# Modulation sums of the first layer on TensorE's column groups, inside the loop of the first projections

## The chip, the cores and the metric

The kernel runs on one core of a Trainium2 chip. The metric is device microseconds from one launch to its end; the median of 3 runs of the kernel before is 2728.34 us (2719.16 to 2734.02). One more execution was profiled: 2728.04 us, of which 2726.2 us lie between its first and its last instruction (the span), so 1.8 us lie around the span. All times below that carry a start are counted from the start of that span. TensorE does the matrix products (PE in the profile, its weight loads PEld), VectorE is DVE, ScalarE is ACT, GpSimd is POOL; SP issues most of the transfers (DMA) from the main memory.

## The reference

Two layers over x of 1024 positions by 2048 features, float32. Only the head of layer 0 is touched:

```python
cond = jax.nn.silu(c)                              # c: (1, 2048)
mod = cond @ w_mod[layer] + b_mod[layer]           # w_mod[0]: 2048 x 6144
shift, scale, gate = jnp.split(mod[:, None, :], 3, axis=-1)
h = rms_norm(x, ln_pre_g[layer]) * (1.0 + scale) + shift
...
proj = h @ w_in                                    # 2048 x 7168, parts a_u a_v a_z q k v b_z
out_a = spatial_gating(gelu(a_u), gelu(a_v), ...) * silu(a_z)
out_b = stick_breaking(q, k, v) * silu(b_z)        # 8 heads of 128, causal, 128-query blocks
x = x + gate * rms_norm(concat(out_a, out_b) @ w_out_ab, ln_post_g)
```

The shift part and the scale part of w_mod[0] are 2048 by 2048 numbers each, 16.8 MB each, and are read once for one vector times matrix product. Layer 1 (a state space layer) is not touched.

## The kernel before

Matrix products run at float32 accuracy by splitting both factors into a rounded part and a rest (`split`, L179: ACT makes the rounded part `whi`, DVE or POOL the rest `wlo`), and three products per tile (`mm3`, L205 to L208). h is kept transposed, features on the partitions, in two halves of 512 positions: `hTh[0]`, `hTl[0]` and `hTh[1]`, `hTl[1]`, 16 tiles k of 128 features each. A projection of 256 output columns takes its weights in pieces of 4 k (1024 numbers per partition, the tile `wraw`, 3 buffers), cut into two splits.

The head of the program, in its order:

1. The first half of x is loaded (`xa`, 4 transfers) and then six small vectors (`rows`), all by SP; one transpose makes columns of them, and ACT makes `cond`.
2. `x_norm` (L313): ACT squares and sums each of the 4 row blocks, `rstd_from` gives the factors, ACT and DVE scale.
3. The scale part of the modulation in six column groups (L352): 16 transfers of 1 MB through three slots of `raw0`; DVE multiplies each k row by `cond` and accumulates (`matvec`, L174); a product with a vector of ones sums over the partitions (`col_sums`, L158); `scale_shift` makes `asc`. Then `h_tile` (L327) transposes x, and ACT and DVE write hTh and hTl, without the shift. Between these groups the first half of six banks (three projections, called `first`: b_z of two heads, q with k, a_u with a_z) is accumulated, k by k, with weights that GpSimd's queue loads and whose rests GpSimd makes.
4. The second half of x (`xb`) is loaded, normed, transposed; the shift part of the modulation is summed by DVE in four column groups (L403, tiles `m`); the second half of the first two projections follows (`bz0e`, `qk0e`).
5. `add_shift` (L343) adds the shift to all 32 tiles of h and splits them again; what `first` lacked is repaired later: `bias_first` (L438) loads the six weight columns again and forms shift times weights on DVE, the products `pbias`, and biases for b_z, u, z, q, k.
6. `proj_v` of head 0 (`v0e`, both halves), the second half of the third projection (`uz0e`), and then the loop over the 8 heads: projections of the next head fill TensorE between the small steps of the attention of the current one (`z`, `oT`). The chunks of the other modulation parts run on DVE in heads 0 to 2 (`mod_chunk`).

The order on each engine is made by the scheduler of the framework from priorities (`hi_prio`) and the data's dependences. Each engine runs its list in order; SP and GpSimd issue transfers in order, and an issue that waits for a buffer holds all behind it.

Of the kernel before, what the change touches and what calls it, by code (L numbers as in the profile page):

```python
# [19 lines left out]
KT = 16  # L20
# [43 lines left out]
def hybrid_trunk(ctx: ExitStack, tc: tile.TileContext, x, c, ln_pre_g, ln_post_g, w_mod, b_mod,  # L64
# [52 lines left out]

    xa = big_tile(1, [128, 4, D], F32, "xa")
    for t in range(4):
        dma(out=xa[:, t, :], in_=x[0, t * 128:(t + 1) * 128, :])  # L120
    with tc.tile_pool(name="p0r", bufs=1) as p0r:
        rows = p0r.tile([128, 128], F32, name="rows")
        dma(out=rows[0:16], in_=flat_rows(c[0], 16))
        dma(out=rows[16:48], in_=ln_pre_g.rearrange("l (r p) -> (l r) p", p=128))
        for i in range(2):
            dma(out=rows[48 + 32 * i:80 + 32 * i], in_=flat_rows(b_mod[i, 0:4096], 32))
        dma(out=rows[112:120], in_=flat_rows(sgu_norm_g[0], 8))
        dma(out=rows[120:128], in_=flat_rows(b_glu[0], 8))
# [3 lines left out]
    tab.begin("silu")  # L132
    tab.act(cond, cols[:, 0:16], AF.Silu)
# [49 lines left out]
    def load_raw(parts, ncols, dma=dma):  # L183

        raw = wp.tile([128, RAW], F32, tag="wraw", name="wraw")
# [78 lines left out]
    pu = []  # L264
    pq_stack = ctx.enter_context(ExitStack())
    pq = pq_stack.enter_context(pool("pq"))
    wv0 = w_mod[0].rearrange("(k p) n -> p k n", p=128)
    bias0 = const.tile([128, 6], F32, name="bias0")

# [9 lines left out]
    def new_uz():  # L279
        st["u"], st["z"] = (pu[0].tile([128, L], F32, tag=n, name=n) for n in ("u", "zg"))  # L280

    def evac_bz(cb, hf, ps):
        S.activation(perm(st["bz"][cb])[:, hf * 64:(hf + 1) * 64, :], ps.rearrange("p (n j) -> p n j", j=8), AF.Copy)

    def evac_qk(cb, hf, ps):
        S.activation(st["qk"[cb]][:, hf * 512:(hf + 1) * 512], ps, AF.Copy,
                     scale=(1.0 / math.sqrt(HD) if cb == 0 else 1.0))

    def evac_qk0(cb, hf, ps):
        S.activation(st["qk"[cb]][:, hf * 512:(hf + 1) * 512], ps, AF.Copy)  # L290

    def evac_uz(cb, hf, ps):
        S.activation(st["uz"[cb]][:, hf * 512:(hf + 1) * 512], ps, AF.Copy)
# [9 lines left out]
    new_bz()  # L303
    new_qk()
    with pool("p0") as p0:
        tab.begin("explog")
        rb = big_tile(1, [128, 8192], F32, "raw0")
        hTh[0] = big_tile(0, [128, KT, 512], F32R, "hTh0")
        hTl[0] = big_tile(0, [128, KT, 512], F32R, "hTl0")
        xs_ = [[xa[:, t, :] for t in range(4)]]  # L310
        junk0 = p0.tile([128, D], F32, tag="xb", name="junk0", bufs=4)

        def x_norm(xt, junk, n):  # L313
            ss = p0.tile([128, 4], F32, tag=f"ss{n}", name=f"ss{n}")
            for t in range(4):
                S.activation(junk, xt[t], AF.Square, accum_out=ss[:, t:t + 1])
            r = rstd_from(ss, 4, D, p0, f"r{n}")
            for t in range(4):
                if t % 2 and n == 0:
                    V.tensor_scalar(out=xt[t], in0=xt[t], scalar1=r[:, t:t + 1], scalar2=None, op0=ALU.mult)  # L320
                else:
                    S.activation(xt[t], xt[t], AF.Copy, scale=r[:, t:t + 1])

        x_norm(xs_[0], junk0, 0)
        ps6 = [mm_tile("first") for _ in range(4)] + [ps_z.tile([128, 512], F32, tag="z", name="first") for _ in range(2)]

        def h_tile(hf, k):  # L327
            pz = xbank[k % 3] if hf and k % 3 < 2 else ps_t.tile([128, 512], F32, tag="t", name="xT")
            for i in range(4):
                T.transpose(pz[:, i * 128:(i + 1) * 128], xs_[hf][i][:, k * 128:(k + 1) * 128], ident)  # L330
            sc = asc[:, 0, k:k + 1]
            S.activation(hTh[hf][:, k, :], pz, AF.Copy, scale=sc)
            lo = hTl[hf][:, k, :]
            if hf == 0:
                V.scalar_tensor_tensor(out=lo, in0=pz, scalar=sc, in1=hTh[hf][:, k, :], op0=ALU.mult, op1=ALU.subtract)
            else:
                tmp = p0.tile([128, 512], F32, tag="ht", name="ht", bufs=2)
                S.activation(tmp, pz, AF.Copy, scale=sc)
                G.tensor_tensor(out=lo, in0=tmp, in1=hTh[hf][:, k, :], op=ALU.subtract)

        hsb = []

        def add_shift(hf, k):  # L343
            if not hsb:
                hsb.append(p0.tile([128, 4, 512], F32, tag="xb", name="hs", bufs=4))
            tmp = hsb[0][:, k % 4, :]
            V.scalar_tensor_tensor(out=tmp, in0=hTh[hf][:, k, :], scalar=shf[:, 0, k:k + 1], in1=hTl[hf][:, k, :],
                                   op0=ALU.add, op1=ALU.add)
            split(hTh[hf][:, k, :], hTl[hf][:, k, :], tmp, (V, G)[k % 2])

        nm = 0
        for kb, (ka, kz) in enumerate(((0, 1), (1, 2), (2, 4), (4, 8), (8, 12), (12, 16))):  # L352
            n = (kz - ka) * 128
            acc = rb[:, 6144 + (kb % 2) * 512:6144 + (kb % 2) * 512 + n]
            kn = 2048 // n
            for k0 in range(0, KT, kn):
                m = rb[:, (nm % 3) * 2048:(nm % 3 + 1) * 2048].rearrange("p (k n) -> p k n", k=kn)
                nm += 1
                last = dma(out=m, in_=wv0[:, k0:k0 + kn, D + ka * 128:D + kz * 128])
                for ki in range(kn):  # L360
                    matvec(acc, m[:, ki, :], k0 + ki)
            pcs = ps_o.tile([128, kz - ka], F32, tag="o", name="cs")
            col_sums(pcs, acc, kz - ka)
            scale_shift(0, slice(ka, kz), pcs, None, p0)
            with hi_prio():
                for k in range(ka, kz):
                    h_tile(0, k)
            if kb == 0:
                after = last.ins
                with hi_prio(), tc.issue_after(after):  # L370
                    raws = [load_raw(src_ab(*first[0], 0)(0, 4), 256)]
            if kb < 2:
                continue
            if kb == 2:
                with hi_prio(), tc.issue_after(last.ins):
                    raws += [load_raw(src_ab(*f_, 0)(0, 4), 256) for f_ in first[1:]]
            for gi, (s0, s1) in enumerate(first):
                k0 = kz - 4
                src = src_ab(s0, s1, 0)(k0, k0 + 4)
                for wh, wl in load_w(src, 256, G, raws[gi] if kb == 2 else None, G.dma_start):  # L380
                    for kk in range(2):
                        for cb in range(2):
                            mm3(ps6[gi * 2 + cb], *opT(k0 + kk, wh[:, kk], wl[:, kk], cb, 0), k0 + kk == 0, k0 + kk == KT - 1)
                    k0 += 2
        evs = (evac_bz, evac_qk0)
        for gi in range(2):
            for cb in range(2):
                with hi_prio():
# [939 lines left out]
```

## Time and profile before

| what | value |
|---|---|
| median of 3 runs | 2728.34 us |
| profiled execution, its span | 2728.04 us, 2726.2 us |
| TensorE busy in the span | 2595.3 us, 95% |
| VectorE busy | 1733.9 us, 64% |
| granted TensorE clock, mean | 0.986 of full speed |
| last product of `first` starts | 145.62 us |
| first product of `v0e`, of `uz0e` starts | 231.94 us, 286.99 us |

A matmul's record lasts longer than the time it holds the array, since the next one starts before it ends: the distance from one start to the next is the price when the array is full. A product of two float32 operands is two instructions in the trace, a product of split operands is one.

### The profile page before, as it was taken

Reading aid. Unit: us, or ns where it says so; the run is one execution under the profiler, and the core shown is the slowest. Engines: PE = TensorE matmul, PEld = TensorE weight load, DVE = VectorE, ACT = ScalarE, POOL = GpSimd, SP = SyncE. Lnnn points to the kernel's source line nnn. Section 1 sums busy time; section 2 is a strip of 40 time slices with the busy share of each in tenths; the row PEclk is TensorE's granted clock in tenths of the full one; section 3 lists DMA queues with packets and bytes.
Section 4 is the critical chain, followed back from the end, with each engine's and each line's share of the span. In section 5 each row is a group of like instructions: output and inputs, shape, how many; then the busy total and the mean of one; then the engine's idle time right before and its main releaser. Section 6 shows DMA issues by size and latency. Waiting matters only on the chain.

```text
span 2726.2 us, 38501 instructions
## 1 busy us (share of the span) xinstructions
PE 2595.3 (95%) x13639; PEld 2180.4 (80%) x13639; DVE 1733.9 (64%) x3783; ACT 1029.2 (38%) x2035; POOL 487.8 (18%) x771
## 2 busy tenths in 40 slices
PE   4878999999999999999999999999999999999998
PEld 3667988988988878878889777777877888887876
DVE  7798876666776666765847663455364768446354
ACT  3444552433424234334334353444352321134333
POOL 2375000000001162441613400020030000002000
PEclk9889999999999999999999999999999999999999
DMA  8764746375482232422413335453254676363354
GB/s 279 269 209 117 220 148 217 124 237 175 156 261 66 73 101 70 122 73 68 137 45 115 103 105 189 147 178 108 99 191 154 206 220 199 118 205 139 131 193 165
DMA packets 357311, 417.95 MB, mean 153 GB/s; under 512 B 23760, under 2 KB 239104, under 8 KB 355712
## 3 DMA queue, kind: packets, MB, share of 16 engines
q1 hardware_dynamic: 347568, 392.95, 45.1%
q0 software_dynamic: 9552, 22.56, 2.5%
q8 instruction: 107, 1.75, 0.3%
q14 instruction: 84, 0.69, 0.1%
HBM read 355.62 MB, written 59.79 MB: 152 GB/s over the span
## 4 chain that ended last, share of the span: by engine, by line
PE 68%; DVE 11%; DMA 8%; issue 8%; ACT 3%; POOL 1%; SPq 0%; DVEq 0%; ACTq 0%; POOLq 0%
PE oT L580 2%; PE z L552 2%; DVE acc L174 2%; DMA mraw<-in_w_mod_dram 2%; PE o0e L206 2%; PE o1e L206 2%; PE o1e L208 2%; PE o1e L207 2%; PE o0e L208 2%; PE o0e L207 2%; DVE wlo L181 1%; DMA xr<-in_x_dram 1%; DMA wraw<-cat_d 1%; PE su1e L206 1%; PE wT_ps L576 1%
## 5 line engine op out<-in xcount | busy, mean ns | idle before, releaser
L180 ACT ACTIVATE whi<-wraw 128x512 fp32r<-128x512 f32 x632 | 395.2, 629 | 997.8 <-PE o1e L208 91.3
L181 DVE TENSOR_TENSOR wlo<-wraw,whi 128x512 fp32r<-128x512 f32 x592 | 420.8, 714 | 486.3 <-ACT whi L180 482.6
L174 DVE SCALAR_TENSOR_TENSOR macc<-mraw,cond,macc 128x512 f32<-128x512 f32 x240 | 180.0, 750 | 67.3 <-DMA mraw<-in_w_mod_dram 62.9
L207 PE MATMUL o1e<-wlo,catH 128*128 128x512 f32 x256 | 101.1, 395 | 4.7 <-DVE wlo L181 4.5
L56 ACT ACTIVATE sp<-sp 128x128 f32<-128x128 f32 (+3 forms) x192 | 99.4, 521 | 3.7
L207 PE MATMUL o0e<-wlo,catH 128*128 128x512 f32 x256 | 100.7, 393 | 0.0
L208 PE MATMUL o1e<-whi,catL 128*128 128x512 f32 x256 | 100.5, 393 | 0.0
L208 PE MATMUL o0e<-whi,catL 128*128 128x512 f32 x256 | 100.2, 393 | 0.0
L206 PE MATMUL o0e<-whi,catH 128*128 128x512 f32 x256 | 90.9, 398 | 7.9 <-ACT whi L180 3.9
L904 POOL TENSOR_TENSOR gt<-gt,zt 128x1024 f32<-128x1024 f32 x8 | 20.0, 2511 | 430.6 <-DMA gt<-g_d 430.6
L206 PE MATMUL o1e<-whi,catH 128*128 128x512 f32 x256 | 88.1, 395 | 2.2 <-ACT jk L704 2.0
L56 ACT ACTIVATE sp<-z 128x128 f32<-128x128 f32 (+3 forms) x96 | 46.6, 486 | 110.0 <-PE z L552 109.0
L735 POOL DMA_DIRECT2D x_d<-y x32 | 17.9, 561 | 369.7 <-DVE y L732 368.3
L580 PE MATMUL oT<-wT,v 128*128 128x128 f32 x576 | 81.1, 277 | 0.7 <-DVE wT L578 0.7
L174 DVE SCALAR_TENSOR_TENSOR acc<-m,cond,acc 128x512 f32<-128x512 f32 x60 | 74.6, 1243 | 7.9 <-DMA m<-in_w_mod_dram 6.5
L580 PEld LDWEIGHTS oT<-wT,v 128*128 128x128 f32 x576 | 75.9, 193 | 4.0 <-DVE wT L578 1.1
L552 PE MATMUL z<-k,q 128*128 128x128 f32 (+3 forms) x192 | 77.3, 486 | 0.6 <-DVE wt L569 0.6
L56 ACT ACTIVATE wt<-wt 128x128 f32<-128x128 f32 (+3 forms) x96 | 50.2, 523 | 62.5 <-DVE wt L569 62.2
L557 DVE SCALAR_TENSOR_TENSOR sp<-z,sp 128x128 f32<-128x128 f32 (+3 forms) x96 | 52.9, 551 | 31.6 <-ACT sp L56 31.5
L181 POOL TENSOR_TENSOR wlo<-wraw,whi 128x512 fp32r<-128x512 f32 x40 | 59.8, 1510 | 65.9 <-ACT whi L180 64.4
L578 DVE COPY wT<-wT_ps 128x128 f32<-128x128 f32 (+3 forms) x96 | 53.1, 553 | 28.8 <-PE wT_ps L576 28.3
L559 POOL TENSOR_SCALAR_AFFINE_SELECT sp<-sp 128x128 f32<-128x128 f32 x64 | 25.3, 395 | 257.0 <-DVE sp L557 240.7
(634 smaller groups left out, 8100.1 us busy)
## 6 DMA issues: line engine op xcount, KB each, us to landing
wraw<-in_w_in_ab_dram SPq DMA_DIRECT2D x268, 256.0 KB, 3.3
mraw<-in_w_mod_dram SPq DMA_DIRECT2D x256, 256.0 KB, 3.7
wraw<-in_w_in_ssm_dram SPq DMA_DIRECT2D x56, 512.0 KB, 4.4
wraw<-in_w_out_ab_dram SPq DMA_DIRECT2D x48, 512.0 KB, 3.7
raw<-in_w_mod_dram SPq DMA_DIRECT2D x16, 1024.0 KB, 6.2
m<-in_w_mod_dram SPq DMA_DIRECT2D x32, 512.0 KB, 4.4
wraw<-in_w_out_ssm_dram SPq DMA_DIRECT2D x32, 512.0 KB, 3.7
wraw<-in_w_in_ab_dram SPq DMA_DIRECT2D x17, 512.0 KB, 4.8
```

The source lines that it names most:

```text
L56: r = self.nc.scalar.activation(out, in_, func, **kw)
L174: V.scalar_tensor_tensor(out=acc, in0=m, scalar=cond[:, k:k + 1], in1=acc, op0=ALU.mult, op1=ALU.add)
L180: S.activation(h, r, AF.Copy)
L181: eng.tensor_tensor(out=lo, in0=r, in1=h, op=ALU.subtract)
L206: T.matmul(ps, sh, mh, start=first, stop=False)
L207: T.matmul(ps, sh, ml, start=False, stop=False)
L208: T.matmul(ps, sl, mh, start=False, stop=last)
L552: T.matmul(z[:, :w], q[:, i * 128:(i + 1) * 128], kT[:, k0:k1], start=True, stop=True)
L557: V.scalar_tensor_tensor(out=a[:, :w], in0=z[:, :w], scalar=0.0, in1=a[:, :w], op0=ALU.max, op1=ALU.add)
L576: T.transpose(pt[:, j * 128:(j + 1) * 128], b[:, j * 128:(j + 1) * 128], ident)
L578: V.tensor_copy(wT[:, :w], pt[:, :w])
L580: T.matmul(oT, v[:, k0 // 128 + j, :], wT[:, j * 128:(j + 1) * 128], start=nb_done == 0, stop=nb_done == i)
```

## The change

Step 3 to 5 are rewritten. The condition vector is repeated 32 times in columns (`condb`, 128 x 16 x 32), and w_mod's rows are streamed through TensorE against it: four products of 32 output partitions, each in another column group of the array (`prow[32j:32j+32]`), the groups 0 and 1 for the scale (even and odd k), 2 and 3 for the shift. The row sums are copied by ACT (`srow`) and turned into columns by a product with a selecting matrix `sel`, which also adds the groups. Scale and shift of two k tiles (a block, 8 blocks in all) are so known together, and `h_tile` writes h with its shift: the repair by `add_shift` and `bias_first` goes, and so do `bias0` and the scaling that waited for it. A block takes 4 transfers of 1 MB in 8 slots (`rb` and `ring2`), and every second block takes three weight pieces (`load_raws`), which land in `wraw` or in the buffers of bz0, bz1 and k; all are issued by SP, two blocks ahead. The small vectors move to ACT's queue. PE, ACT, DVE and SP follow the written order in this loop (`manual_schedule`), all splits are on DVE. After it `v0e` of the first half is put ahead of `bz0e` and `qk0e`, and `v0e` of the second half behind them.

```diff
     xa = big_tile(1, [128, 4, D], F32, "xa")
-    for t in range(4):
-        dma(out=xa[:, t, :], in_=x[0, t * 128:(t + 1) * 128, :])
...
-        dma(out=rows[0:16], in_=flat_rows(c[0], 16))
+        S.dma_start(out=rows[0:16], in_=flat_rows(c[0], 16))
...
+        with tc.manual_schedule(engines={mybir.EngineType.SP}), hi_prio():
+            for t in range(4):
+                xlast = dma(out=xa[:, t, :], in_=x[0, t * 128:(t + 1) * 128, :])
...
-        def add_shift(hf, k):
...
+        def h_tile(hf, k, xt, pz):
...
+            S.activation(hi, pz, AF.Identity, scale=sc, bias=sh)
+            full = xt[:, :, cs]
+            S.activation(full, pz.rearrange("p (a b) -> p a b", a=4), AF.Identity, scale=sc, bias=sh)
+            V.tensor_tensor(out=hTl[hf][:, k, :].rearrange("p (a b) -> p a b", a=4), in0=full,
+                            in1=hi.rearrange("p (a b) -> p a b", a=4), op=ALU.subtract)
...
+        def load_chunks(b, half):
+            for i in range(2):
+                slot = (4 * b + 2 * half + i + 4) % 8
...
+                    st["last"] = dma(out=m, in_=wv0[:, half * 8:half * 8 + 8, c0:c0 + 256])
...
+        def sums(b, half):
+
+            for k in range(0, 8, 2):
+                for j in range(4):
+                    m = chunk[b, half, 1 - j // 2]
+                    kk = half * 8 + k + j % 2
+                    T.matmul(prow[32 * j:32 * j + 32], condb[:, kk, :], m[:, k + j % 2, :],
+                             start=kk < 2, stop=kk >= KT - 2)
...
+            for b in range(NB):
+                old = dict(wpair)
+                sums(b, 0)
+                if b + 2 < NB:
+                    load_chunks(b + 2, 0)
+                if b:
+                    for gi in range(3):
+                        first_mm(b - 1, 0, gi, old[gi])
+                sums(b, 1)
+                if b + 2 < NB:
+                    load_chunks(b + 2, 1)
+                    if b % 2 == 0:
+                        load_raws(b + 2)
+                srow = pu.tile([128, 256], F32, tag="u", name="srow")
+                S.activation(srow, prow, AF.Copy)
+                if b:
+                    first_mm(b - 1, 1, 0, old[0])
+                ks = slice(2 * b, 2 * b + 2)
+                cs = hd[:, 256:260].rearrange("p (k s) -> p k s", s=2)
+                for i in range(2):
+                    T.matmul(cs[:, i, :], srow[:, i * 128:(i + 1) * 128], sel, start=True, stop=True)
+                scale_shift(0, ks, cs[:, :, 0], cs[:, :, 1], p0)
+                split_w(b, 0)
+                h0(2 * b)
+                for gi in (1, 2):
+                    if b:
+                        first_mm(b - 1, 1, gi, old[gi])
+                    split_w(b, gi)
+                h0(2 * b + 1)
...
-        for kb in range(4):
-            acc = p0.tile([128, 512], F32, tag="acc", name="acc0", bufs=2)
...
+        proj_v(0, 0)
...
-        proj_T(0, *first[0], evac_bz, "bz", ((1,),), G)
-        proj_T(0, *first[1], evac_qk0, "qk", ((1,),), G)
-        for hf in range(2):
-            for k in range(KT):
-                add_shift(hf, k)
+        proj_T(0, *first[0], evac_bz, "bz", ((1,),))
+        proj_T(0, *first[1], evac_qk, "qk", ((1,),))
+        proj_v(0, 1)
...
-        def bias_first():
...
-        bias_first()
```

On PE, in the middle of the head: before, a group's column sums (`cs`), one transpose of x and then the products of `first` on that tile; numbers behind a name tell buffers apart.

```order
L207 MATMUL first<-hTl_136,whi 128x512
L208 MATMUL first<-hTh_135,wlo 128x512
L158 MATMUL cs<-ones,raw_134 128x1 x4
L206 MATMUL first<-hTh_135,whi 128x512 x4
L330 MATMUL xT<-ident,xa 128x128 x4
L207 MATMUL first<-hTl_136,whi 128x512
L208 MATMUL first<-hTh_135,wlo 128x512
```

And now, the middle of block 1: sums of its second half (`mrow`), products of block 0's second tile, the columns (`sel`), a transpose, and products again.

```order
L384 MATMUL mrow_154<-raw0_143,condb_147 32x256 x16
L213 MATMUL first_148<-hTh0_145,whi_250 128x512
L214 MATMUL first_148<-hTl0_146,whi_250 128x512
L215 MATMUL first_148<-hTh0_145,wlo_251 128x512
L213 MATMUL first_149<-hTh0_145,whi_250 128x512
L214 MATMUL first_149<-hTl0_146,whi_250 128x512
L215 MATMUL first_149<-hTh0_145,wlo_251 128x512
L436 MATMUL mrow_154<-sel_102,srow_332 128x2 x2
L353 MATMUL xT_350<-ident_91,xa_108 128x128 x4
L213 MATMUL first_150<-hTh0_145,whi_262 128x512
L214 MATMUL first_150<-hTl0_146,whi_262 128x512
L215 MATMUL first_150<-hTh0_145,wlo_263 128x512
```

The column sums were eight short instructions behind work of DVE; now 16 products of 32 output partitions each stand twice in a block between the products of `first`, and all of them use TensorE. The tile of which `first` is multiplied is one block older than the sums.

On DVE, at the same place: before, the accumulation of the modulation (L174) with the small steps and the rest of an h tile between.

```order
L174 SCALAR_TENSOR_TENSOR raw_134<-raw_134,cond 128x512 x4
L335 SCALAR_TENSOR_TENSOR hTl_136<-xT,asc,hTh_135 128x512
L174 SCALAR_TENSOR_TENSOR raw_134<-raw_134,cond 128x512 x7
L172 TENSOR_SCALAR raw_134<-raw_134,cond 128x512
L174 SCALAR_TENSOR_TENSOR raw_134<-raw_134,cond 128x512 x3
L164 TENSOR_TENSOR sct<-cs,cols 128x4
L174 SCALAR_TENSOR_TENSOR raw_134<-raw_134,cond 128x512
L165 SCALAR_TENSOR_TENSOR asc<-sct,cols 128x4
L174 SCALAR_TENSOR_TENSOR raw_134<-raw_134,cond 128x512
L335 SCALAR_TENSOR_TENSOR hTl_136<-xT,asc,hTh_135 128x512
```

Now, one block: the columns of scale and shift, three rests of weights, two rests of h.

```order
L170 TENSOR_TENSOR sct<-mrow,cols 128x2
L171 SCALAR_TENSOR_TENSOR asc<-sct,cols 128x2
L174 TENSOR_TENSOR shf<-mrow,cols 128x2
L187 TENSOR_TENSOR wlo<-wraw,whi 128x512
L359 TENSOR_TENSOR hTl_146<-xa,hTh_145 128x512
L187 TENSOR_TENSOR wlo<-wraw,whi 128x512 x2
L359 TENSOR_TENSOR hTl_146<-xa,hTh_145 128x512
```

No accumulation is left on DVE there; the rests of the weights have come to it from POOL.

On SP, from the start: before, x, the small vectors, then the modulation's chunks with the first weight pieces between.

```order
L120 DMA xa<-in_x_dram 128x2048 x4
L123 DMA rows<-in_c_dram 16x128
L124 DMA rows<-in_ln_pre_g_dram 32x128
L126 DMA rows<-in_b_mod_dram 32x128 x2
L127 DMA rows<-in_sgu_norm_g_dram 8x128
L128 DMA rows<-in_b_glu_dram 8x128
L359 DMA raw_134<-in_w_mod_dram 128x16x128
L188 DMA wraw<-in_w_in_ab_dram 128x4x256
L359 DMA raw_134<-in_w_mod_dram 128x16x128
L359 DMA raw_134<-in_w_mod_dram 128x8x256 x2
L188 DMA wraw<-in_w_in_ab_dram 128x4x128 x4
L359 DMA raw_134<-in_w_mod_dram 128x4x512 x12
```

Now:

```order
L136 DMA xa<-in_x_dram 128x2048 x4
L375 DMA ring_144<-in_w_mod_dram 128x8x256 x4
L195 DMA wraw<-in_w_in_ab_dram 128x4x256
L195 DMA wraw<-in_w_in_ab_dram 128x4x128 x4
L375 DMA raw_143<-in_w_mod_dram 128x8x256 x4
L375 DMA ring_144<-in_w_mod_dram 128x8x256 x4
L195 DMA fraw<-in_w_in_ab_dram 128x4x256
L195 DMA fraw<-in_w_in_ab_dram 128x4x128 x4
```

The chunks start right behind x, each group of four is a block, and the weight pieces (`wraw`, `fraw`) stand behind every second one. The other pieces, which POOL issued before, are on SP now.

## Rows read from the trace of the kernel before

**Rows 1.** The page, part 2: TensorE busy and granted clock in 40 equal slices of the span.

```profile
PE   4878999999999999999999999999999999999998
PEclk9889999999999999999999999999999999999999
```

**Rows 2.** Busy time by stage: stretch, length, engines (instructions), granted clock, DMA share, GB/s.

```profile
core 0: us, PE busy (x) PEld busy (x) DVE busy (x) ACT busy (x) POOL busy (x), PEclk, DMA share, GB/s
0.00:146.00 146.00, 93.18 (x399) 73.27 (x400) 104.39 (x165) 61.90 (x78) 48.95 (x47) 0.92 0.80 277
146.00:232.00 86.00, 65.30 (x278) 50.41 (x276) 79.47 (x69) 39.78 (x67) 64.55 (x38) 0.86 0.52 161
232.00:287.00 55.00, 49.20 (x392) 48.39 (x391) 42.37 (x69) 22.99 (x49) 19.38 (x13) 0.97 0.60 173
```

**Rows 3.** Waits of PE, first 400 us: who waited for whom, us, times, longest.

```profile
PE cs L158 <- DVE acc L174: 11.4, 4, 7.3
PE cs L158 <- DVE raw L174: 10.5, 2, 6.3
PE first L208 <- POOL wlo L181: 8.5, 2, 7.7
```

**Rows 4.** Groups by shape, first 300 us, DVE: xcount, busy us, mean ns of one.

```profile
L174 DVE SCALAR_TENSOR_TENSOR acc<-m,cond,acc 128x512 f32<-128x512 f32 x60 | 74.6, 1243 | 7.9 <-DMA m<-in_w_mod_dram 6.5
...
L174 DVE SCALAR_TENSOR_TENSOR raw<-raw,cond 128x512 f32<-128x512 f32 x45 | 43.4, 967 | 1.0
```

**Rows 5.** Timeline of PE, three places: start us, record's us, instruction.

```profile
53.99 0.60 PE L330 MATMUL xT<-ident,xa 128*128 128x128 f32 x4
54.34 0.49 PE L207 MATMUL first<-hTl,whi 128*128 128x512 f32 x1
...
286.75 0.28 PE L207 MATMUL v0e<-wlo,hTh 128*128 128x256 f32 x1
286.87 0.28 PE L208 MATMUL v0e<-whi,hTl 128*128 128x256 f32 x1
...
287.23 0.40 PE L207 MATMUL uz0e<-hTl,whi 128*128 128x512 f32 x1
287.46 0.39 PE L208 MATMUL uz0e<-hTh,wlo 128*128 128x512 f32 x1
```

**Rows 6.** Timeline of PE at 344 us: a float32 product (z) between split ones.

```profile
344.23 1.02 PE L552 MATMUL z<-k,q 128*128 128x512 f32 x2
344.69 0.68 PE L208 MATMUL v1e<-whi,hTl 128*128 128x256 f32 x1
345.21 0.28 PE L206 MATMUL v1e<-whi,hTh 128*128 128x256 f32 x1
```

**Rows 7.** Timeline of PE at 979 us: a float32 product with 32 output partitions (k_ps).

```profile
979.04 0.39 PE L207 MATMUL qk4e<-hTl,whi 128*128 128x512 f32 x1
979.36 0.41 PE L1282 MATMUL k_ps<-s5cAr,s5bd 128*32 128x128 f32 x2
979.69 0.50 PE L208 MATMUL qk4e<-hTh,wlo 128*128 128x512 f32 x1
980.03 0.40 PE L206 MATMUL qk4e<-hTh,whi 128*128 128x512 f32 x1
```

**Rows 8.** Busy time of two stretches with full transfer queues: last columns DMA share, GB/s.

```profile
4.00:12.00 8.00, 0.00 (x0) 0.00 (x0) 0.00 (x0) 5.33 (x5) 0.00 (x0) 1.00 1.01 424
32.00:42.00 10.00, 9.23 (x29) 6.98 (x30) 9.71 (x23) 1.32 (x2) 1.56 (x1) 1.00 1.08 375
```

**Rows 9.** Timeline of ACT: the square of the last row block of xa.

```profile
13.26 1.91 ACT L316 ACTIVATE junk<-xa 128x2048 f32<-128x2048 f32 x1 [0.58 <-DMA xa<-in_x_dram]
```

**Rows 10.** Groups by shape, first 300 us, ACT.

```profile
L180 ACT ACTIVATE whi<-wraw 128x512 fp32r<-128x512 f32 x63 | 38.9, 627 | 56.4 <-PE first L207 24.5 <-PE v0e L208 15.5 <-issue 5.4
L332 ACT ACTIVATE hTh<-xT,asc 128x512 fp32r<-128x512 f32 x32 | 21.9, 685 | 54.1 <-PE xT L330 34.3 <-DVE asc L165 19.7
...
L322 ACT ACTIVATE xb<-xb,r 128x2048 f32<-128x2048 f32 x4 | 7.7, 1996 | 2.1 <-DVE r L151 2.1
...
L316 ACT ACTIVATE raw<-xb 128x2048 f32<-128x2048 f32 x4 | 7.6, 1906 | 0.0
```

More of the change, by code (lines that the diff above doesn't have):

```diff
@@ L314, in x_norm, with silu_c @@
+        def silu_c():
+            sig = p0.tile([128, KT], F32, tag="sig", name="sig")
+            tab.act(sig, cols[:, 0:16], AF.Exp, scale=-1.0)
+            V.tensor_scalar(out=sig, in0=sig, scalar1=1.0, scalar2=None, op0=ALU.add)
+            V.reciprocal(out=sig, in_=sig)
+            V.tensor_tensor(out=cond, in0=cols[:, 0:16], in1=sig, op=ALU.mult)
+            V.tensor_copy(condb, cond.unsqueeze(2).to_broadcast([128, KT, 32]))
+        def x_norm(xt, junk, n, between=None):
             ss = p0.tile([128, 4], F32, tag=f"ss{n}", name=f"ss{n}")
@@ L324, in hybrid_trunk @@
-        x_norm(xs_[0], junk0, 0)
+                if t % 2:
+                    V.tensor_scalar(out=xt[:, t, :], in0=xt[:, t, :], scalar1=r[:, t:t + 1], scalar2=None, op0=ALU.mult)
+                else:
+                    S.activation(xt[:, t, :], xt[:, t, :], AF.Copy, scale=r[:, t:t + 1])
         ps6 = [mm_tile("first") for _ in range(4)] + [ps_z.tile([128, 512], F32, tag="z", name="first") for _ in range(2)]
-        def h_tile(hf, k):
-            pz = xbank[k % 3] if hf and k % 3 < 2 else ps_t.tile([128, 512], F32, tag="t", name="xT")
+        def h_tile(hf, k, xt, pz):
+            cs = slice(k * 128, (k + 1) * 128)
@@ L341, in hybrid_trunk @@
-        hsb = []
-        def add_shift(hf, k):
[L344 to L384, printed above, removed]
@@ new lines, in h0 @@
+        def h0(k):
+            h_tile(0, k, xa, ps_t.tile([128, 512], F32, tag="t", name="xT"))
+        order = {mybir.EngineType.PE, mybir.EngineType.Activation, mybir.EngineType.DVE, mybir.EngineType.SP}
+        with tc.manual_schedule(engines=order), hi_prio():
+            x_norm(xa, rb[:, 6144:8192], 0, silu_c)
+            for b in range(2):
+                for half in range(2):
+                    load_chunks(b, half)
+                if b == 0:
+                    load_raws(0)
+            for b in range(NB):
[27 more added lines that the diff above has]
+                h0(2 * b + 1)
@@ new lines, in hybrid_trunk @@
+        new_bz()
+        new_qk()
+        new_uz()
+        evs = (evac_bz, evac_qk, evac_uz)
+        with tc.manual_schedule(engines={PE, mybir.EngineType.Activation}), hi_prio():
+            for gi in range(3):
+                for kk in range(2):
+                    first_mm(NB - 1, kk, gi, wpair[gi])
+                for cb in range(2):
+                    done = evs[gi](cb, 0, ps6[gi * 2 + cb])
+        last = st["last"]
+        xb = p0.tile([128, 4, D], F32, tag="xb", name="xb")
+        for t in range(4):
@@ L401, in hybrid_trunk @@
-        for k in range(KT):
-            h_tile(1, k)
-        for kb in range(4):
-            acc = p0.tile([128, 512], F32, tag="acc", name="acc0", bufs=2)
-            for kq in range(8):
-                m = p0.tile([128, 2, 512], F32, tag="m0", name="m0", bufs=3)
-                with tc.issue_after(last.ins):
-                    dma(out=m, in_=wv0[:, kq * 2:(kq + 1) * 2, kb * 512:(kb + 1) * 512])
-                for ki in range(2):
-                    matvec(acc, m[:, ki, :], kq * 2 + ki)
-            pcs = ps_o.tile([128, 4], F32, tag="o", name="cs")
-            col_sums(pcs, acc, 4)
-            scale_shift(0, slice(kb * 4, kb * 4 + 4), None, pcs, p0)
@@ L628, in hybrid_trunk @@
                 proj_T(h, 6, None, evac_bz, "bz")
[L629 to L630 removed]
+            if h not in (0, 2, 4):
+                for hf in range(2):
+                    proj_v(h, hf)
             gate_a(h - 1)
```

176 lines of the change are left out of this document (72 added, 104 removed).

## The prediction

> **What bounds the kernel now.** I read the 40 slices first [rows 1]: TensorE is at 9 tenths from the fifth slice on, so behind about 290 us the time is TensorE's own work, which the change leaves as it is. A gain or a loss can only be a shift of the moment at which that stretch starts. The mark for it is the end of `v0e`, 287.0 us, where `uz0e` follows without a gap. Then I read the head by stages [rows 2]: TensorE is busy 93.2 of the first 146 us, 65.3 of the next 86 and 49.2 of the last 55, in all 207.7 of 287 us, and part of that at the lower clock (mean 0.92 and 0.86). VectorE is busy 104.4 and 79.5 us in the first two stages. The waits [rows 3] name it: column sums wait for the accumulation (11.4 and 10.5 us), products wait for rests that GpSimd makes (8.5 us). The accumulation alone takes 74.6 us for 60 steps of the shift part and 43.4 us for 45 steps of the scale part [rows 4]. So VectorE sets the head's pace, and transfers come second: 277 GB/s in the first stage where full queues reach 375 to 424 [rows 2, 8].
>
> **Prices.** A split product with 512 columns costs 0.23 us from start to start (I use 0.227, three in 0.68), one with 256 columns 0.12, four transposes 0.35 [rows 5]. A float32 product with 512 columns costs 0.98 - 0.12 = 0.86 us, as two instructions [rows 6]; with 256 columns it is half, 0.43. Going into a product of 32 output partitions and out again is not free [rows 7]: `k_ps` starts 0.09 us later than the product before it needs, its two instructions of 128 columns take 0.33 us where a quarter of the 0.86 would be 0.21, and the next product takes 0.34 instead of 0.23. That is 0.09 + 0.12 + 0.11 = 0.32 us for a visit.
>
> **What goes.** The 105 accumulations, GpSimd's rests, `add_shift` with its second split of 32 tiles, and the reload of 6.3 MB for the repair. None of them is a gain by itself: what is late next decides, and that is either the transfers or TensorE.
>
> **Transfers.** The two parts of w_mod (33.5 MB) and the weights of `first` (6.3 MB) now come in one row behind x. x is in at 13.2 us [rows 9]; the small vectors leave SP's queue, and their six issues lie on ACT's, before and between squares that wait for x anyway. At 375 GB/s, the rate where rows of 1 KB and shorter ran [rows 8], a block's 4.19 MB take 11.2 us, two blocks' weights (1.57 MB) 4.2 us, so a block costs 13.3 us and the last chunk lands at 13.2 + 39.8/0.375 = 119 us. The first half of block 1 is in at 13.2 + 11.2 + 4.2 + 5.6 = 34.2 us. SP waits for a slot until the sums two blocks earlier are done, so it stays ahead as long as TensorE is the slower of the two.
>
> **TensorE's block.** 36 products of `first`: 8.2 us. Eight transposes: 0.7. The selection, two float32 products of two columns: 0.4, an estimate below the 0.33 of a `k_ps` pair each. Two visits to the 32 partition form: 0.64. And 32 float32 products of 256 columns for the sums. No row of this trace shows two column groups at work together, so this term has two ends: each for itself 32 x 0.43 = 13.7 us; all four groups together, a quarter, 3.4 us. I take the half, 6.8 us. The reason lies in rows 6 and 7: a float32 product is two instructions in the same columns of the array, and PE's rows start in the order of the program. The second instruction of one group must follow the first, so only it and the first instruction of the next group can run side by side. A block is then 8.2 + 0.7 + 0.4 + 0.64 + 6.8 = 16.8 us, more than the transfers' 13.3: TensorE sets the pace.
>
> The Trainium skill (TensorE: Matmul & The Clock Gate, Part 3: Packing small matmuls) says that matmuls keep strict program order in start and end, and gives a measured 2.38 times for three column groups. By that factor, stretched to four groups (3.2), the sums would be 4.3 us and the time about 2687 us; it does not say that its products were pairs, as those here are [rows 6], and no run here shows it yet.
>
> **What lies beside TensorE's block.** ACT: a copy of the sums, three rounded weights at 0.63, four passes over h tiles at 0.69 [rows 10], about 5 us. VectorE: five rests at some 0.7 and three small steps, about 4.5 us. Both fit in 16.8. The chain from the sums to the columns (copy, selection, three small steps, ACT, rest) has the products of the tile before as cover, 1.4 us under the copy and 2.7 under the rest, and the tiles made in block b are first used after the next sums. I charge it nothing; without the cover it would be about 3 us a block, 21 in all.
>
> **Sum to the end of the first stage.** Block 0's chain ends before block 1 has its chunks. From 34.2 us: 2 us for a spell of some 4 us at half clock (an estimate; the mean of 0.92 in rows 2 is 23 us at half clock in 146), seven blocks of 16.8 = 117.6, the last block's products 8.2. That is 162.0 us, where before the last product of `first` is issued at 145.6. This stage becomes longer, but the shift is in it.
>
> **From there to the end of `v0e`.** TensorE: 384 products at 0.12 = 46.1, 192 at 0.227 = 43.6, 64 transposes 5.6, in all 95.3 us. The norm of the second half of x starts only behind the last evacuation: squares 4 x 1.9, factors about 2.5, two scalings 4.0 on ACT, with four rounded weights between, some 19 us; the first half of `v0e` (23 us) covers it. The 16 tiles need two ACT passes each (22 us), and with 8 rounded weights and the evacuations of `v0e` ACT is full for 51 us, while TensorE would be through at 50: the products of `bz0e` end some 6 us late. So 102 us, and `v0e` ends at 264.0 instead of 287.0. Before, this work took from 145.9 to 287.0, 141 us. Behind it nothing differs by more than single rows, no product waits longer, and VectorE has less to do.
>
> Result: 2728.0 - 23.0 = **2705 us**. The profiled execution (2728.04) is at the median of the runs (2728.34), so no offset.
>
> **Rivals.**
> *The four groups run fully together.* A block is 8.2 + 0.7 + 0.4 + 0.64 + 3.4 = 13.4 us, equal to the transfers. First stage: 36.2 + 7 x 13.4 + 8.2 = 138 us; `v0e` ends at 240; time 2681. For it speaks that the code alternates the groups in its innermost loop, against it the pairs [rows 6].
> *The groups don't overlap: slower.* Each sum waits for the one before. The sums cost 13.7 us a block, the block is 23.6, the first stage ends at 36.2 + 165.2 + 8.2 = 209.6, `v0e` at 311.6, 24.6 us later than now: 2753. It turns slower than before once a block is above 16.8 + 23/7 = 20.1 us, that is, when the sums take over 10.1 us or 0.32 us each. What speaks for it: `k_ps` [rows 7] shows a pair that did not even follow its neighbours without gaps. Against: it has one group only.
> *The clock eats the gain.* If in the loop the granted clock is as low as the 0.86 of the second stage [rows 2], 117.6 us become 137: 19 us, time 2724, the same as before. For it: waits at the start and the many changes of form; against: TensorE has work without long gaps, and where it had [rows 1] the clock was full. Transfers at the first stage's 277 GB/s [rows 2] would give a smaller loss: last chunk at 157 us, about 16 us of chain and products behind it, time 2716.
>
> **How the numbers follow.** Forecast (half overlap) 50%, its own range 2693 to 2718 from the chain's 0 to 1.5 us a block and `v0e`'s end 4 us either way. Full overlap 23%. No overlap 15%. Clock or transfers 12%. Half a per cent, 13.6 us, is about what can be told from no change: 2714 to 2742 is the same. Of the forecast's half 0.41 is faster and 0.09 same; full overlap is all faster; no overlap 0.13 slower, 0.02 same; the last case 0.02 faster, 0.07 same, 0.03 slower. Faster 0.66, same 0.18, slower 0.16. The range from 2674 to 2742 leaves out no overlap and the ends of the others.
>
> **What would show it.** In the profile after: `mrow` groups of 16 starting 0.21 us apart on average (0.43: no overlap, 0.11: full); a block's period, from one `srow` to the next, near 16.8 us; a granted clock near 1 from 40 us on; the last `first` near 162 us and the first `uz0e` of the second half near 264. Waits of `mrow` for chunks in most blocks would say that transfers set the pace. I am wrong if the period is above 20 us, if PE waits for `asc` or hTl inside the loop, or if the stretch behind 290 us itself changes by more than 5 us.

## The result and the profile after

Four runs of each on one chip: 2695.6 us median (2689.6 to 2700.1) where the kernel before took 2725.8 (2719.2 to 2734.0). The ratio is 0.9886, 95% interval 0.9848 to 0.9924: faster by some 30 us, 1.1%, clear of the noise. The profiled execution took 2689.6 us, 38 less than the one of before; it is the fastest of its four.

The page after, busy tenths and granted clock in 40 slices:

```profile
span 2687.9 us, 39058 instructions
PE   6999999999999999999999999999999999999998
PEclk9999999999999999999999999999999999999999
```

TensorE is at 9 tenths from the second slice on, where before it came there in the fifth [rows 1]. The time behind the head is still TensorE's own. The two stages of the new head, up to the end of the first products and up to the end of `v0e`, and the loop itself (stretch, length, engines with instructions, clock, DMA share, GB/s):

```profile
0.00:141.00 141.00, 115.22 (x897) 80.73 (x898) 35.67 (x84) 58.37 (x85) 0.70 (x6) 0.98 1.01 355
141.00:246.00 105.00, 100.36 (x647) 90.51 (x645) 46.82 (x76) 59.13 (x98) 2.39 (x5) 0.98 0.44 134
```
```profile
30.00:45.00 15.00, 11.46 (x89) 7.06 (x90) 3.06 (x5) 4.29 (x7) 0.00 (x0) 0.77 1.09 385
45.00:117.00 72.00, 72.00 (x582) 52.28 (x581) 19.71 (x45) 27.64 (x44) 0.00 (x0) 1.00 1.06 362
```

VectorE is busy 82 of 246 us, before 226 of 287 [rows 2]. From 45 to 117 us TensorE has no idle time at all and the full clock, while the transfers run at 362 GB/s. The rows of ACT's copies of the sums give the loop's period (start, length, [idle before <- what ended it]):

```profile
58.23 0.38 ACT L430 ACTIVATE srow<-mrow 128x256 f32<-128x256 f32 x1 [6.69 <-PE mrow L384]
...
71.88 0.38 ACT L430 ACTIVATE srow<-mrow 128x256 f32<-128x256 f32 x1 [6.69 <-PE mrow L384]
...
85.52 0.38 ACT L430 ACTIVATE srow<-mrow 128x256 f32<-128x256 f32 x1 [6.69 <-PE mrow L384]
```

13.65 us a block, to a hundredth, where the forecast was 16.8. PE's rows around one half of the sums say why:

```profile
83.46 1.93 PE L384 MATMUL mrow<-ring,condb 128*32 128x256 f32 x32
85.33 0.50 PE L213 MATMUL first<-hTh,whi 128*128 128x512 f32 x1
```

16 calls, 32 instructions, are through in 1.87 us. The trace's single records show four starts within 20 ns, the next four 0.24 us later, and each further set 0.2155 us behind the one before: eight sets, 1.72 us, and some 0.14 for going in and out. A set of four costs what one instruction of a float32 product costs by itself (half of the 0.43 that the prediction took from [rows 6]). So the four groups run fully together.

PE's waits in the head (us, times, longest):

```profile
PE mrow L384 <- DMA ring<-in_w_mod_dram: 8.7, 2, 6.9
PE v0e L214 <- DVE wlo L187: 3.3, 1, 3.3
PE mrow L384 <- DMA raw<-in_w_mod_dram: 2.1, 1, 2.1
...
PE qk0e L215 <- DVE wlo L187: 1.4, 1, 1.4
PE first L214 <- DVE hTl L359: 0.9, 1, 0.9
```

The waits of [rows 3] are gone. What is left are waits for the first chunks (block 0 and the first half of block 1), 0.9 us in the last block's products, and two waits in the second stage that were not foreseen. VectorE's rows there show where they come from:

```profile
214.00 0.75 DVE L180 SCALAR_TENSOR_TENSOR macc<-mraw,cond,macc 128x512 f32<-128x512 f32 x1 [2.31 <-DMA mraw<-in_w_mod_dram]
214.67 0.68 DVE L187 TENSOR_TENSOR wlo<-wraw,whi 128x512 fp32r<-128x512 f32 x1
...
221.30 0.75 DVE L180 SCALAR_TENSOR_TENSOR macc<-mraw,cond,macc 128x512 f32<-128x512 f32 x1 [2.44 <-DMA mraw<-in_w_mod_dram]
221.97 1.29 DVE L187 TENSOR_TENSOR wlo<-wraw,whi 128x512 fp32r<-128x512 f32 x2
```

The accumulations for the later modulation chunks (`mod_chunk`) now begin before `v0e` ends; each stands in VectorE's queue waiting for its own transfer, and the rest `wlo` that PE needs stands behind it.

The gain along the program, profile against profile:

```profile
245.53 0.40 PE L213 MATMUL uz0e<-hTh,whi 128*128 128x512 f32 x1
```

`uz0e` starts at 245.5 us instead of 287.0, 41.5 us earlier; the first product of head 0's output projection (`o0e`) at 1566.4 instead of 1605.3; the span ends 38.3 us earlier. The gain is made in the head and kept. What goes is idle time: TensorE stood idle 79.3 of the first 287 us [rows 2] and now 30.4 of 246, while its busy time rises from 207.7 to 215.6. The clock has a share that is not told apart: the means of 0.92, 0.86 and 0.97 [rows 2] have become 0.98, by these figures up to some 20 us of TensorE's time (an estimate, and the most, since it counts idle time as well).

The medians show less than the profiles: 30 us here, and 33 in a second set of runs (2687.8 against 2720.9, below). In all experiments the median falls 4 to 12 us less than the end of `v0e` moves against the one profiled execution of before. That execution took 2728.0 us, where the medians of before beside the experiments are 2720 to 2724, so some of the 41.5 us may belong to it and not to the change; the runs do not tell how much.

### The profile page after: what moved, and what is told of

The parts are those of the page before. It is cut to its first block, busy times and chain, and to the rows that moved or that the text cites. A ratio compares the mean times of both kernels' runs of the same rounds, so it can differ in the third digit from the quotient of the medians.

```text
span 2687.9 us, 39058 instructions
## 1 busy us (share of the span) xinstructions
PE 2604.1 (97%) x14107; PEld 2178.7 (81%) x14107; DVE 1576.0 (59%) x3597; ACT 1022.6 (38%) x2021; POOL 361.1 (13%) x684
## 4 chain that ended last, share of the span: by engine, by line
PE 73%; DMA 8%; DVE 8%; issue 7%; ACT 2%; SPq 1%; POOL 0%; DVEq 0%; ACTq 0%; POOLq 0%
PE z L566 2%; DMA mraw<-in_w_mod_dram 2%; PE oT L594 2%; DVE wlo L187 2%; PE o1e L213 2%; PE o1e L215 2%; PE o1e L214 2%; DMA wraw<-cat_d 2%; PE o0e L213 1%; PE o0e L215 1%; PE o0e L214 1%; PE mrow L384 1%; PE su1e L213 1%; PE su1e L215 1%; PE su1e L214 1%
## 5 line engine op out<-in xcount | busy, mean ns | idle before, releaser
L186 ACT ACTIVATE whi<-wraw 128x512 fp32r<-128x512 f32 x620 | 389.0, 630 | 988.5 <-PE o1e L215 89.7
L187 DVE TENSOR_TENSOR wlo<-wraw,whi 128x512 fp32r<-128x512 f32 x620 | 438.6, 711 | 506.5 <-ACT whi L186 497.2
L213 PEld LDWEIGHTS o0e<-whi,catH 128*128 128x128 f32 x256 | 49.0, 192 | 21.1 <-ACT jk L706 6.3
L1274 ACT ACTIVATE s5wb<-wb_ps 128x128 f32<-128x128 f32 x64 | 17.7, 276 | 119.3 <-DVE s5wb L1273 108.4
```

The costliest lines, as they stand in the source:

```text
L186: S.activation(h, r, AF.Copy)
L187: eng.tensor_tensor(out=lo, in0=r, in1=h, op=ALU.subtract)
L213: T.matmul(ps, sh, mh, start=first, stop=False)
```

## The experiments

**What lets the groups overlap.** In `sums`, the order of the 16 calls of a half alone is changed. One group after the other:

```
-            for k in range(0, 8, 2):
-                for j in range(4):
+            for j in range(4):
+                for k in range(0, 8, 2):
```

> The loop over the four column groups goes outside the loop over rows, so that four calls of one group follow each other; the work is the same. Theory (products run side by side only where neighbours in the order of the program lie in different groups, and TensorE sets the loop's pace): of 32 instructions of a half only those at the three borders between groups overlap, 29 x 0.2155 = 6.2 us for a half instead of 1.86, block 13.65 + 2 x 4.35 = 22.3 us, total 2696 + 7 x 8.7 + 4.3 = 2761 us, above the kernel before. Rival (the array sorts the groups itself, or the loop's pace is not TensorE's): block stays at 13.65 us and the time at 2696.

Measured: 1.0023 of before (1.0010 to 1.0036), so the whole gain is lost, but only about half of the loss expected came. Block 18.97 us (its copies start at 69.32, 88.29, 107.27). PE's rows of one half:

```profile
93.73 4.59 PE L384 MATMUL mrow<-ring,condb 128*32 128x256 f32 x32
98.25 0.50 PE L213 MATMUL first<-hTh,whi 128*128 128x512 f32 x1
```

4.52 us, neither 6.2 nor 1.87. Two windows on the same place, up to 94.62 and up to 94.64 us, show how:

```profile
93.73 1.27 PE L384 MATMUL mrow<-ring,condb 128*32 128x256 f32 x5
```
```profile
93.73 1.30 PE L384 MATMUL mrow<-ring,condb 128*32 128x256 f32 x6
```

The single records start at 93.731, 93.971, 94.187, 94.402, 94.618 (the first group, 0.24 us and then 0.2155 us apart) and 94.624. The records do not name their group; that the last one is of another is read from the 6 ns, and from its length, 0.403 us like the very first one's, where those behind a product of their own group have 0.379. So the second group begins with the first one's fifth instruction, while three of the first are still to come (the sixth starts at 94.834). The third group begins 0.893 us after the second, the fourth 0.894 us after the third. 3 x 0.893 + 8 x 0.2155 + 0.12 = 4.52. That is no matter of neighbours. It looks as if instructions are handed out in the program's order, one in each group runs, up to three more can wait behind it, and only a fourth holds up those of other groups. Each product has a weight load of its own in front of it (PEld); whether it is the product or its load that waits is not told apart here. This reading was then put to the test by two more orders.

Two groups in turn, then the other two:

```
+            for jj in (0, 2):
                 for k in range(0, 8, 2):
-                for j in range(4):
+                    for j in (jj, jj + 1):
```

> The calls alternate between two groups, first groups 0 and 1 for all rows, then 2 and 3; the work is the same. This makes the half overlap that the prediction took. Theory: sets of two, each 0.2155 us, 16 sets = 3.45 us for a half (3.6 with the visit), block 13.65 + 2 x 1.72 = 17.1 us, first stage 8 x 3.45 = 26 us longer, total about 2722. Rival 1 (a pair's second instruction can run beside the next group only, so that two groups do no better than one): half 6.2 us, as with one group at a time, total 2761. Rival 2 (pace from elsewhere): 13.65 us, 2696.

Measured: 0.9938 (0.9919 to 0.9957), 2701.1 us; block 15.42 us.

```profile
82.39 2.82 PE L385 MATMUL mrow<-ring,condb 128*32 128x256 f32 x32
85.15 0.50 PE L213 MATMUL first<-hTh,whi 128*128 128x512 f32 x1
```

A half takes 2.75 us: theory and both rivals missed. The reading above gives 0.90 + 1.72 + 0.12 = 2.74: groups 2 and 3 begin at 83.295 us, right behind the fifth instructions of groups 0 and 1 (83.282, 83.289).

Two calls, four instructions, of one group behind each other:

```
-            for k in range(0, 8, 2):
-                for j in range(4):
+            for k0 in range(0, 8, 4):
+                for j in range(4):
+                    for k in (k0, k0 + 2):
```

> Two calls (four instructions) of one group follow each other before the next group's; the work is the same. With one group at a time the next group began 0.893 us after the one before, while the fifth of its eight instructions ran (4.52 us for a half). Theory (issue runs ahead: up to three instructions wait in their group behind the one that runs, and do not stop those of other groups): runs of four cost nothing, a half stays at 1.87 us, block 13.65 us, time as changed, some 0.989 of before. Rival (a group must be through with half of its run before the next starts): 0.43 us for each change of group, half about 3.5 us, block 16.9 us, 23 us more. Second rival (only neighbours at the border of two groups overlap): half 5.4 us, block 20.7 us, 50 us more.

Measured: 0.9882 (0.9864 to 0.9900), as the changed kernel; block 13.72 us.

```profile
77.93 1.97 PE L385 MATMUL mrow<-ring,condb 128*32 128x256 f32 x32
79.83 0.50 PE L213 MATMUL first<-hTh,whi 128*128 128x512 f32 x1
```

1.90 us: runs of four cost 0.03 us a half. Both rivals fall, and all four orders (four groups in turn in runs of two, four and eight instructions, and two groups in turn) fit one reading.

**Does TensorE set the loop's pace?** Each product of the sums twice (the selecting ones become 0.5):

```
             for k in range(0, 8, 2):
+                for r in range(2):
...
```

> Each product of the sums is issued twice (the column of ones that selects the rows holds 0.5 instead), still alternating over four groups. Theory (TensorE sets the loop's pace without slack): the half takes 3.6 instead of 1.86 us, block 17.1 us, total 2696 + 8 x 3.45 = about 2722. Rival (transfers set the pace and TensorE's added work lies in waits for chunks): block under 14.5 us, total under 2704.

Measured: 0.9987 (0.9976 to 0.9998), 2717.9 us; block 17.10 us, half 3.59 us.

```profile
89.32 3.66 PE L385 MATMUL mrow<-ring,condb 128*32 128x256 f32 x64
92.91 0.50 PE L213 MATMUL first<-hTh,whi 128*128 128x512 f32 x1
```

Twice 1.72 us a block came and twice 1.72 us are seen: nothing hides work on TensorE in this loop. The sums of this kernel (7.2 us a block) are near the 6.8 that the prediction took, its block 17.10 near 16.8; so this is nearly the kernel that was forecast, and it is only 3 us faster than before, not 23. And half of the sums:

```
-            for k in range(0, 8, 2):
+            for k in range(0, 8, 4):
...
```

> Leaves out every second pair of rows of the sums (the chunks are still loaded), so the modulation of layer 0 is not the reference's. TensorE's block falls by 2 x 0.86 to 11.9 us. Theory (transfers are just behind TensorE): the block ends at the transfers' 4.97 MB / 375 GB/s = 13.3 us, PE now waits for chunks, total 2 to 4 us less, 2692 to 2694. Rival (transfers have room to run faster when slots come free earlier): block 11.9 to 12.3 us, total 10 to 13 us less, 2683 to 2686.

Measured: 0.9872 (0.9856 to 0.9888), 2684.9 us. ACT's copies:

```profile
42.91 0.38 ACT L430 ACTIVATE srow<-mrow 128x256 f32<-128x256 f32 x1 [9.58 <-PE mrow L384]
...
54.84 0.38 ACT L430 ACTIVATE srow<-mrow 128x256 f32<-128x256 f32 x1 [4.95 <-PE mrow L384]
...
69.59 0.38 ACT L430 ACTIVATE srow<-mrow 128x256 f32<-128x256 f32 x1 [7.77 <-PE mrow L384]
...
122.52 0.38 ACT L430 ACTIVATE srow<-mrow 128x256 f32<-128x256 f32 x1 [5.82 <-PE mrow L384]
```

Without a wait a block is 11.93 us (42.91 to 54.84), but every second one waits for chunks (five waits, 9.1 us), and the mean of six is 79.61/6 = 13.27 us: 4.97 MB in that time are 375 GB/s, the price of the prediction. So transfers are 0.38 us a block behind TensorE, and at this rate of transfers less work on TensorE can bring no more than that. The first products end 4.0 us earlier, at 136.9 us, and the median is 3 us below that of the changed kernel where both stand against 2721 us of before (2687.8, below): the 2 to 4 us of the theory. That the absolute time lies in the rival's band comes from the base of 2696, which is from another set of runs.

**Does the first half of `v0e` cover the norm?** It is moved behind `qk0e`:

```
-        proj_v(0, 0)
         xbank = [...]
...
-        proj_v(0, 1)
+        for hf in range(2):
+            proj_v(0, hf)
```

> The first half of v0e, which needs nothing of the second half of x, moves from ahead of bz0e to behind qk0e; the work is the same. Theory (v0e's first half covers the norm of x's second half): TensorE stands idle from the end of the first stage (141 us) to the first tile of the second half, 159 us, so +18 us and about 1 us at half clock behind the gap: time 16 to 20 us above the changed kernel, about 0.996 of before. Rival (the cover is not needed, since ACT's passes over the tiles set the pace of this part anyway): under 4 us more.

Measured: 0.9945 (0.9927 to 0.9962), 2704.5 us, 17 more than the kernel with two calls in a row on the same chip.

```profile
PE xT L353 <- ACT xb L345: 12.9, 2, 12.5
```
```profile
142.00:158.00 16.00, 3.52 (x13) 2.71 (x14) 4.00 (x8) 14.03 (x16) 0.00 (x0) 0.59 0.06 22
158.00:165.00 7.00, 7.00 (x30) 5.59 (x30) 3.71 (x6) 6.62 (x11) 0.00 (x0) 0.72 0.00 0
```

TensorE waits 12.9 us, not 18: with no weights to round between the norm's steps ACT begins its scalings at 152.06 us instead of 154.50, and the first transposes start at 154.1. But the mean clock is 0.59 and 0.72 over 16 and 7 us (from 154.1 to 162.0, with work at hand, 0.51: the lower of the two levels, 1.2 GHz), and `v0e` ends 19.4 us later. Of these, 14.1 us are more waits in the second stage (18.8 against 4.7 in the changed kernel). The other 5.3 go with the clock; by the 0.51, an estimate, 3.9 of them lie before 162 us. The cover is real, and the clock was a larger part of the price than the 1 us expected.

**What held the head before?** The kernel before with VectorE's accumulations of the shift left out but for eight:

```
-                for ki in range(2):
+                for ki in range(2 if kq == 0 else 0):
```

> The kernel before, without 56 of the 64 accumulations of the shift part (the chunks are still loaded), so the shift of layer 0 is not the reference's. Theory (VectorE set the pace of the head): some 65 us of VectorE's work go, the end of v0e moves from 287 to below 267 us, time at least 20 us less, under 0.993 of before. Rival (transfers, or the chain over GpSimd and ACT, hold the head anyway): end of v0e moves by less than 6 us, time within 6 us of before.

Measured: 0.9997 (0.9985 to 1.0008). In the profile VectorE is busy 180 instead of 226 us of the first 287, `v0e` ends 10 us earlier, and the median shows nothing; 10 us is about what profile and median differ by in the other runs too. PE's waits in its head:

```profile
PE xT L330 <- ACT xa L322: 10.3, 2, 9.1
PE cs L158 <- DVE raw L174: 9.3, 2, 6.2
PE first L208 <- POOL wlo L181: 8.1, 2, 7.2
PE first L206 <- ACT whi L180: 7.9, 3, 6.6
PE qk0e L208 <- POOL wlo L181: 5.0, 4, 2.2
```

PE waits as long as before for VectorE's scale part and for x (19.6 us; before 19.4), and 13.1 us for rests that GpSimd makes (12.1 before). So in the next run these go to VectorE too:

```
-                for wh, wl in load_w(src, 256, G, raws[gi] if kb == 2 else None, G.dma_start):
+                for wh, wl in load_w(src, 256, V, raws[gi] if kb == 2 else None):
```

and `proj_T` of `bz` and `qk` without its last argument `G`.

> The kernel before without 56 of the 64 accumulations of the shift part, as in the run before, and the rests of the weights of first, bz0e and qk0e on VectorE instead of GpSimd, their loads on SP's queue instead of GpSimd's (the shift of layer 0 is not the reference's). Taking VectorE's accumulations alone moved the end of v0e from 287 to 277 us in the profile and left the median where it was. Theory (VectorE and GpSimd held the head together: with VectorE freed, the products wait for GpSimd's rests): waits for GpSimd's rests (13 us) go, the end of v0e comes below 265 us, time 0.992 of before or less. Rival (what holds the head is the order of its chain: column sums in six steps, tiles, products, then the same tiles once more for the shift): the end of v0e stays above 272 us, time 0.997 to 1.003 of before.

Measured: 0.9903 (0.9878 to 0.9928), 2695.1 us; the first products end at 131.1 us, `v0e` at 248.7.

```profile
PE cs L158 <- DVE raw L174: 8.5, 2, 4.3
PE xT L330 <- ACT xa L322: 8.1, 2, 6.9
PE v0e L207 <- DVE wlo L181: 7.2, 3, 4.0
PE qk0e L208 <- DVE wlo L181: 5.1, 6, 1.7
```

38 us of the head, nearly the 41.5 that the change gave, and 28.6 us in the median. GpSimd's rests have gone from the waits. VectorE freed alone shows nothing in the median. GpSimd freed alone was not tried, so that both held the head together is not shown; an estimate speaks for it: VectorE is busy 177.2 of the first 249 us here, and with the 56 accumulations at 1.243 us [rows 4] it would be 246.8, which leaves no room. The run also moves the loads of these weights from GpSimd's queue to SP's, and what of the gain is theirs is not told apart.

**A better order.** Two moves on the changed kernel, put to the test together, then the first alone, then the changed kernel and both moves side by side:

```
             wv = w_mod[layer].rearrange("(k p) n -> p k n", p=128)
+            if (layer, n0) == mods[0]:
+                V.tensor_copy(acc[:, 0:1], st["v"][:, 7, 0:1])
...
                 for half in range(2):
                     load_chunks(b, half)
-                if b == 0:
-                    load_raws(0)
+                    if b == 1 and half == 0:
+                        load_raws(0)
```

The copied column is overwritten at once; it only makes the first accumulation wait for the last evacuation of `v0e`.

> The changed kernel with two moves: the first accumulation for the later modulation chunks waits for the last evacuation of v0e, so that no rest of a weight stands behind it on VectorE, and the weights of block 0 and 1 are loaded behind the third of the first four pairs of chunks. Theory: the two waits of PE for rests (1.4 and 3.3 us) go, and the sums of block 1 start some 4 us earlier while the products behind them wait for the weights, so 1 to 2 us there; together 4 to 6 us less than the changed kernel, 0.987 of before. Rival (the accumulations come in the way of the attention of head 0 later, or of its loads): no gain, within 2 us.

> Of the two moves in the mended order only one: the first accumulation for the later modulation chunks waits for the last evacuation of v0e; the weights of blocks 0 and 1 are loaded where the changed kernel loads them. Theory (all of the 7 us came from this one, since the first stage ended at 141.5 us in the mended order and at 140.9 in the changed kernel): v0e ends at 239 us, time 0.985 to 0.986 of before. Rival (the weights' move gave part of it): 0.987 of before or more, v0e ends above 242 us.

> The changed kernel once more, on one chip with the next, so that the two stand side by side. Theory: some 0.988 of before; v0e ends at 245 us.

> The mended order (both moves) once more, beside the changed kernel. Theory: the 7 us between the ends of v0e (239 against 245.5) are there in the medians too, 0.9975 of the changed kernel. Rival: the difference lies within what differs from chip to chip, under 2 us here.

Measured, in this order: both moves 0.9855 (0.9839 to 0.9870); the first alone 0.9863 (0.9845 to 0.9880), `v0e` to 238.3 us. Side by side on one chip, the changed kernel 2687.8 us (0.9878, 0.9857 to 0.9900) and both moves 2677.2 us (0.9836, 0.9820 to 0.9852). The stretch from the first products to the start of `uz0e`, in the last of these:

```profile
141.00:240.00 99.00, 99.00 (x650) 89.98 (x649) 36.49 (x61) 60.01 (x99) 2.38 (x5) 1.00 0.35 102
```

Both waits are gone, TensorE is busy 99.00 of 99 us, and the clock is 1.00 instead of 0.98; `v0e` ends at 238.8 us, 6.4 earlier than beside it. The weights' move gave nothing that can be seen: the first products end at 141.1 against 140.9 us. Of the 10.6 us between the medians 6.4 are shown in the head; the other 4.2 are not explained and lie within what kernels differ by behind it (from the start of `uz0e` to the end of the span 2434 to 2449 us in these profiles).

## Why the prediction was right, and where not

Direction and range were right: 2695.6 us against 2705. TensorE sets the loop's pace, as described; one term was mis-sized, for a reason that does not hold, and one hold-up was not seen. That 2705 comes nearer than the 2681 of the rival whose overlap was the true one is luck: the kernel with nearly the forecast block is measured at 2717.9 us, so the forecast counted the sums too dear and the rest too cheap, and the two errors make up for each other in part. The range from 2674 to 2742 held most of the rivals as well.

*The term that failed: sums, 6.8 us a block.* Measured 2 x 1.87 = 3.7. The prediction said that "the second instruction of one group must follow the first, so only it and the first instruction of the next group can run side by side". The first half holds (0.2155 us from one to the next in a group), the second does not: an instruction that waits for its own group does not stop those behind it, up to three such (runs of two, four, eight instructions: 1.87, 1.90, 4.52 us). With it goes the premise that PE's rows start in the order of the program: with one group at a time the first one's sixth instruction starts at 94.834 us, behind the second group's first at 94.624. The rival of full overlap, given 23%, is what happened; it asked for 3.4 us, a 13.4 us block and 2681 us, and got 3.7, 13.65 and 2689.6 in the profile.

*The rest of the block* stood: 8.2 + 0.7 + 0.4 + 0.64 = 9.94 us, measured 13.65 - 3.73 = 9.92.

*First stage.* The first sums of block 1, and the one wait behind them:

```profile
34.65 3.62 PE L384 MATMUL mrow<-raw,condb 128*32 128x256 f32 x32 [2.06 <-DMA raw<-in_w_mod_dram]
38.20 0.50 PE L213 MATMUL first<-hTh,whi 128*128 128x512 f32 x1
...
134.43 0.50 PE L214 MATMUL first<-hTl,whi 128*128 128x512 f32 x1 [0.87 <-DVE hTl L359]
```

Chunks of block 1 at 34.65 us (forecast 34.2); the cold spell cost 3.55 - 1.87 = 1.7 us in the sums of block 1 (2 forecast), clock 1.00 behind it; 34.65 + 1.7 + 7 x 13.65 + 8.2 + 0.9 of a wait = 141.0, measured 141.1. The forecast 162.0 differs by seven times 3.15 us of sums, less the 1 us of the other three terms (chunks 0.45 later, cold spell 0.3 shorter, 0.9 of wait).

*The chain at no charge* was right: from the chunks of block 1 to the last sums PE waits for nothing. The 0.9 us for `hTl` stand behind the loop, in the last block's products, where no sums cover the rest.

*From there to the end of `v0e`, 102 us.* Measured 104.4, but for another reason. That ACT would be full and `bz0e` late by 6 us did not come: with the better order ACT is busy 60.0 of 99 us and PE waits for nothing, and the stretch takes 97.7 us (141.1 to 238.8), 2.4 over the 95.3 counted for TensorE. What came in its place are 4.7 us of rests behind waiting accumulations, and some 2 us of lower clock (0.98 over 105 us, against 1.00). I had written that VectorE has less to do, and did not ask what moves up into its queue.

*VectorE sets the head's pace* was at most part of it: freeing it alone left the median where it was; with GpSimd's rests, and their loads on SP's queue, it was 0.9903. What GpSimd alone would have given stays open.

*No overlap, slower than before.* No order of the calls reaches its 13.7 us: even one group at a time takes 9.0 us a block. The point from which it decides, 20.1 us a block, was too high by some 2 us: at 18.97 us the kernel is already 0.2% slower than before, 4.8 us or 0.6 a block, which puts the point near 18.4 (an estimate).

*Behind 290 us* 41.5 us became 38.3: a change of 3.2, inside the 5 allowed.

## What to carry to other kernels

With small products in several column groups, interleave the groups in the program in runs of at most four instructions; then four groups cost here what one does (1.87 and 1.90 us for a half, against 4.52 in runs of eight). When an engine is relieved, ask what its queue takes in next: an early instruction that waits for its own transfer holds back what another engine needs behind it. And free the second engine of a chain before judging it: VectorE alone showed nothing here, VectorE and GpSimd 28.6 us.

## What was not expected of the hardware

- A group that has an instruction running takes up to three more in waiting before the issue of other groups' instructions stops, as the four orders are read here: next group 0.893 us later in runs of eight, 13 ns later in runs of four.
- With one wait of 12.5 us TensorE's granted clock was 0.59 over the 16 us that hold it and 0.72 over the next 7, though it had work again from 154.1 us on.
